# A hybrid encoder layer: early products from GpSimd to VectorE in pieces, whole-tile activations in halves, x^T staged apart, and the last scores behind the first U tile

## The chip, the cores and the metric

The kernel runs on one core of a Trainium2 chip. The metric is the device time of one execution in microseconds. The kernel before takes 2114.77 us, the median of 3 runs (2113.43 to 2115.89). Engines are named as the profile names them: PE is TensorE (PEld its weight loads), DVE is VectorE, ACT is ScalarE, POOL is GpSimd, and SP is SyncE, which here issues most of the DMAs.

## The reference: one layer on 256 tokens

There are 256 tokens of width 2048, in float32. Cut to what matters:

```
xn   = rms_norm(h, mix_norm_g)
q, k, v, g, xb, yb = split(xn @ w_in)          # six parts of 1024 columns
q, k = rotary(q), rotary(k) * 128**-0.5
ret  = silu(g) * head_group_norm(chunkwise_retention(q, k, v))   # 8 heads of 128

xc   = causal_conv4(xb)                         # RG-LRU, 8 blocks of 128 channels
r, i = sigmoid(xc @ w_rg + b_rg), sigmoid(xc @ w_ig + b_ig)
log_a = 8 * r * log_sigmoid(lru_lambda);  a = exp(log_a)
u    = sqrt(-expm1(2 * log_a)) * (i * xc)
hseq = scan(h_t = a_t * h_(t-1) + u_t)
lru  = rms_norm(hseq * gelu(yb), lru_norm_g)

h += concat(ret, lru) @ w_out
h += cross_attention(rms_norm(h), rms_norm(mem))   # w_xq, w_xk, w_xv, w_xo; 256 memory tokens
h += peer(rms_norm(h))    # 16384 experts: queries w_pq, scores against sub keys, top 16 twice,
                          # then gelu(u_e . x) and v_e of the chosen ones
return rms_norm(h, final_norm_g)
```

## The kernel before

**Weights.** All matrices are float32. SP streams them in half-blocks of 512 KB into four `raw` tiles. `split` (L115) makes two numbers of each weight: ACT casts `hi` (L119, four tiles), and VectorE subtracts to get `lo` (L120, three tiles). The activations are split in the same way: `xT`, `mT`, `cat`, `hT`, `xn` hold a high half [:T] and a low half [T:]. `w_mms` (L123) then issues for a half-block 8 matmuls of `hi` with both halves (L129, 512 columns) and 8 of `lo` with the high half (L131, 256 columns); in the second half-block the last `hi` matmul stands behind the `lo` ones. `col_block` makes a block of 128 output columns from two half-blocks, and `fold` adds the two halves of its result (ACT L153, VectorE L154). `xchunk` does the same with tokens on the partitions (L171, L172 for `hi`, L174 for `lo`).

**Stages.** In order: xb (8 blocks of w_xyg), yb (8 blocks), q, k, v (six chunks), gT (8 blocks), the memory keys w_xk (16 blocks into `kv`) and values w_xv, w_out, w_xq with attention, w_xo, the PEER queries w_pq (16 blocks into `qp`, each followed two blocks later by `sub_scores`), then the U and V tables.

**Side work.** Everything else comes from generators that a `Weave` runs: after each half-block `whalf` pumps `wv.rate` credits (1.1 in the early stages), and the generator at the head of the list is advanced until the credits are used; what it yields is the price of the step in credits. `prep_mem` and `lru` are queued in the yb stage, `retention` in the gT stage, `normed` and `route` later. Within this, a scheduler places the instructions on each engine, each engine then runs its own row in order, and waits where an operand or a buffer is not ready.

**The places that the change touches.** `load_x` (L237) brings a quarter of x^T through a `raw` tile; the four are mixed with the two half-blocks of the first weight block. `prep_mem` scales the memory tokens on GpSimd (L391, 128x1024, four times) and splits them with a gain (`split_gx`, ACT L222 and VectorE L223). In `lru`, GpSimd makes i * xc for all blocks (L329, 128x2048), ACT one square root of 128x2048 (L331); then for each block VectorE clips and inverts (L334, L335), GpSimd multiplies (L336), VectorE adds (L339); GpSimd multiplies the whole (L342), VectorE turns r into a (L344 to L346) and scans (L349, L350). Then ACT applies gelu to all of yb (L355), GpSimd multiplies (L357), ACT squares (L359), TensorE sums over channels (`lss`, L362), and `rsqrt` gives the scale. `lru_fin` applies it in eight products (L376) and splits into `cat`; it is called when the gT blocks are issued. In `retention`, ACT makes the sigmoid of gT (L471) and GpSimd gT * sg (L472), both 128x2048. `sub_scores` (L666) multiplies two 128x128 tiles of `qp` with the keys.

GpSimd's small products (L306, L399, L495, with the row scale of x) and its rotary steps (L427, L432) are not touched.

Of the kernel before, what the change touches and what calls it, by code (L numbers as in the profile page):

```python
# [14 lines left out]
ALU = mybir.AluOpType  # L15
AX = mybir.AxisListType

P = 128
# [53 lines left out]
def hybrid_layer_kernel(ctx: ExitStack, tc: tile.TileContext, a: dict, out: bass.AP, dbg=None):  # L72
# [163 lines left out]

    def load_x(q):  # L237
        t = raw_tile(a["xT"][q]).rearrange("p (k t) -> p k t", t=T)
        split_gx(xT, 4 * q, t, S_MIX)

# [14 lines left out]

    pt0 = mm("w0")
    load_x(0)
    r0 = raw_tile(a["w_xyg"][0, 0])
    load_x(1)
    whalf(0, None, xT, pt0, r0)  # L260
    load_x(2)
    r0 = raw_tile(a["w_xyg"][0, 1])
    load_x(3)
    whalf(1, None, xT, pt0, r0)
    fold(pt0, xb[:, 0, :])
# [11 lines left out]
    def lru():  # L277
# [49 lines left out]
        for g in range(8):  # L327
            A.activation(rt[:, g], rt[:, g], AF.Tanh, scale=lam[:, g:g + 1])
        G.tensor_tensor(it, it, xc, op=ALU.mult)  # L329
        yield 0.3  # L330
        A.activation(xc, rt, AF.Sqrt)  # L331
        yield 5.0
        for g in range(8):
            V.tensor_scalar(xc[:, g], xc[:, g], 1e-18, None, op0=ALU.max)  # L334
            V.reciprocal(q3[:, g], xc[:, g])  # L335
            G.tensor_tensor(q3[:, g], q3[:, g], rt[:, g], op=ALU.mult)  # L336
            yield 2.0
            if g:
                V.tensor_tensor(xc[:, g - 1], xc[:, g - 1], q3[:, g - 1], op=ALU.add)  # L339
        yield 0.4  # L340
        V.tensor_tensor(xc[:, 7], xc[:, 7], q3[:, 7], op=ALU.add)
        G.tensor_tensor(it, it, xc, op=ALU.mult)  # L342
        for g in range(8):
# [9 lines left out]
        while "yb" not in done:  # L353
            yield 3.0
        A.activation(yb, yb, AF.Gelu_apprx_tanh)  # L355
        yield 0.3
        G.tensor_tensor(xc, xc, yb, op=ALU.mult)  # L357
        yield 0.3
        A.activation(q3, xc, AF.Square)  # L359
        pt = sm("lss")  # L360
# [5 lines left out]
        yield 3  # L366
        lru_out.extend([xc, rl])
        done.add("lru")
# [3 lines left out]
    def lru_fin():  # L372
        xc, rl = lru_out
        cat["t"] = ct = big("cat")
        for g in range(8):
            V.scalar_tensor_tensor(xc[:, g], xc[:, g], small[:, S_LG + g:S_LG + g + 1], rl,  # L376
                                   op0=ALU.mult, op1=ALU.mult)
            if g % 4 == 3:
                split_x(ct, 8 + g - 3, xc[:, g - 3:g + 1])

# [3 lines left out]
    def prep_mem():  # L384
# [4 lines left out]
        for q in range(4):  # L389
            t = raw_tile(a["memT"][q]).rearrange("p (k t) -> p k t", t=T)  # L390
            G.tensor_tensor(t, t, rmb[:, None, :].to_broadcast([P, 4, T]), op=ALU.mult)  # L391
            yield 1.0
            split_gx(mT, 4 * q, t, S_MEM)
            yield 2.0
# [20 lines left out]
    def retention():  # L415
# [54 lines left out]
        sg = kt.rearrange("p a (b c) -> p (a b) c", c=T)  # L470
        A.activation(sg, gT, AF.Sigmoid)  # L471
        G.tensor_tensor(gT, gT, sg, op=ALU.mult)  # L472
        yield 0.3
        ct = cat["t"]
# [165 lines left out]
    def normed():  # L640
# [5 lines left out]
        for kb in range(0, KB + 2, 2):  # L646
# [8 lines left out]
            if prev:  # L655
# [3 lines left out]
                yield 0.8  # L659
            prev = nxt  # L660
        for tt in range(TT):
            V.scalar_tensor_tensor(h[tt], h[tt], r2[:, tt:tt + 1], gbc, op0=ALU.mult, op1=ALU.mult)
            yield 2.2
            G.dma_start(hn[tt * P:(tt + 1) * P, :], h[tt])
# [254 lines left out]
    def u_chunk(i):  # L919
        act = acts[i] = tp.tile([P, 8, T], F32, tag="act", name=f"act{i}", bufs=LEAD)  # L920
        for c in range(8):
            pt = mm("U")
            for j in range(2):
                whalf(j, a["U"][8 * i + c, j], xn, pt)
                tick(2 * c + j)
# [366 lines left out]
    for b in range(2, KB):  # L1292
        col_block(a["w_pq"], b, hT2, qp[b // 8][:, b % 8, :])
        sub_scores(b - 2)
    for b in (KB - 2, KB - 1):
        sub_scores(b)
# [146 lines left out]
```

## Time and profile before

| | |
|---|---|
| time, median of 3 runs (us) | 2114.77 (2113.43 to 2115.89) |
| the profiled execution: its own time / span (us) | 2121.89 / 2120.1 |
| mean granted TensorE clock | 0.984 |
| ACT / POOL busy, share of the span | 49% / 19% |
| DMA mean | 256 GB/s |

The stages as the trace has them, from the start of the span: xb to 58 us, yb to 110, q, k, v to 251, gT to 309, w_xk to 430, the PEER queries from about 820 to 913, the U blocks from there. A row of the timeline gives the start, the duration (of the group, where instructions of one form follow each other: x8), the engine, the line, the operation and out<-in; in brackets stands the idle time of the engine ahead of it and what released it. TensorE's granted clock falls after some of its idle times, and matmuls then take longer: `hi` matmuls that are issued 0.23 us apart at full clock are then up to 0.43 apart.

### The profile page before, as it was taken

To read this page: it belongs to the slowest core of one execution; us is meant where nothing else is said; L and a number is where in the kernel's file an instruction comes from. 1 tells how busy PE (TensorE), PEld (TensorE's weight loads), DVE (VectorE), ACT (ScalarE), POOL (GpSimd) and SP (SyncE) were. 2 spreads that over 40 slices of the span, in tenths; PEclk is the share of its full clock that TensorE was granted. 3 is DMA by queue.
4 is the path that set the end of the run, shared out by engine and by line. 5 is a ranking of instruction groups with operands and counts; after the bars stand their busy time and mean duration, and the time that the engine had idled before them with its cause. 6 is when DMAs were issued, how large, how long until landed. Compare 5 with 4: busy or idle time off the path is not lost. (4 is left out here: it accounts for less than half of the span.)

```text
span 2120.1 us, 29007 instructions
## 1 busy us (share of the span) xinstructions
PE 2042.2 (96%) x10452; PEld 1731.5 (82%) x10452; DVE 1701.4 (80%) x2421; ACT 1036.5 (49%) x1592; POOL 393.0 (19%) x211
## 2 busy tenths in 40 slices
PE   8999998999999999999999989999999999988997
PEld 6878787888888888888899978888888888766785
DVE  6857867644554457999997769999999999989897
ACT  6465343444444455554578853434434444433334
POOL 0303212000000000000000002323233332464342
PEclk9999999999999999999999979999999999999999
DMA  8675554566664467555676569999999999999874
GB/s 276 234 224 166 161 189 156 158 190 192 187 187 131 138 187 284 167 177 180 189 275 201 174 221 344 374 386 395 373 363 339 347 382 414 377 362 402 320 257 162
DMA packets 155014, 542.91 MB, mean 256 GB/s; under 512 B 17136, under 2 KB 44400, under 8 KB 136560
## 3 DMA queue, kind: packets, MB, share of 16 engines
q1 hardware_dynamic: 132832, 400.48, 56.2%
q0 software_dynamic: 22032, 140.53, 16.7%
q8 instruction: 82, 1.34, 0.3%
q14 instruction: 68, 0.56, 0.1%
HBM read 541.99 MB, written 18.87 MB: 265 GB/s over the span
## 5 line engine op out<-in xcount | busy, mean ns | idle before, releaser
L120 DVE TENSOR_TENSOR lo<-raw,hi 128x1024 fp32r<-128x1024 f32 x396 | 490.5, 1242 | 279.7 <-PE xc L174 135.1
L119 ACT CAST hi<-raw 128x1024 fp32r<-128x1024 f32 x396 | 414.9, 1050 | 305.6 <-PE xc L172 143.8
L1083 ACT CAST hi<-raw 128x1024 fp32r<-128x1024 f32 x272 | 283.7, 1049 | 266.9 <-DMA raw<-in_V_dram 88.8
L129 PE MATMUL U<-xn,hi 128*128 128x512 f32 x1536 | 403.5, 399 | 7.8 <-ACT hi L119 6.1
L1089 DVE TENSOR_TENSOR lo<-raw,hi 128x1024 fp32r<-128x1024 f32 x272 | 327.7, 1219 | 25.5 <-issue 17.1
L129 PEld LDWEIGHTS U<-xn,hi 128*128 128x128 f32 x1536 | 278.8, 191 | 58.4 <-ACT hi L119 6.2
L1126 POOL DMA_INDIRECT gat<-in_Us_dram,idx x69 | 114.9, 1665 | 684.9 <-DVE gat L1143 419.2
L131 PEld LDWEIGHTS U<-xn,lo 128*128 128x128 f32 x1536 | 212.6, 192 | 16.3 <-DVE lo L1089 1.3
L131 PE MATMUL U<-xn,lo 128*128 128x256 f32 x1536 | 220.8, 285 | 0.4 <-DVE lo L1089 0.4
L1143 DVE SCALAR_TENSOR_TENSOR gat<-gat,h 128x2048 f32<-128x2048 f32 x69 | 157.5, 2283 | 10.3 <-DMA gat<-in_Us_dram,idx 10.3
L944 PE MATMUL acc<-hi,ah 128*128 128x512 f32 x384 | 149.7, 390 | 1.5 <-DVE foldu L928 1.5
L945 PE MATMUL acc<-hi,al 128*128 128x512 f32 x384 | 149.4, 389 | 0.0
L129 PE MATMUL wb<-hT,hi 128*128 128x512 f32 x448 | 119.8, 401 | 0.0
L1126 POOL DMA_INDIRECT gat<-in_Vs_dram,idx x39 | 90.3, 2317 | 128.9 <-DVE hh L1151 111.4
L947 PE MATMUL acc<-lo,ah 128*128 128x512 f32 x384 | 103.4, 391 | 5.4 <-DVE lo L120 3.5
L129 PE MATMUL wb<-xT,hi 128*128 128x512 f32 x368 | 94.8, 399 | 9.8 <-ACT hi L119 9.8
L129 PEld LDWEIGHTS wb<-hT,hi 128*128 128x128 f32 x448 | 81.3, 189 | 14.1
L1151 DVE SCALAR_TENSOR_TENSOR hh<-gat,coef,hh 128x2048 f32<-128x2048 f32 x39 | 91.4, 2344 | 0.1
L947 PEld LDWEIGHTS acc<-lo,ah 128*128 128x128 f32 x384 | 71.6, 188 | 22.5 <-DVE lo L120 4.8
L129 PEld LDWEIGHTS wb<-xT,hi 128*128 128x128 f32 x368 | 67.0, 190 | 23.0 <-ACT hi L119 10.9
L944 PEld LDWEIGHTS acc<-hi,ah 128*128 128x128 f32 x384 | 72.1, 188 | 16.6 <-DVE foldu L928 1.8
L945 PEld LDWEIGHTS acc<-hi,al 128*128 128x128 f32 x384 | 72.1, 188 | 15.0
(410 smaller groups left out, 3722.6 us busy)
## 6 DMA issues: line engine op xcount, KB each, us to landing
raw<-in_U_dram SPq DMA_DIRECT2D x192, 512.0 KB, 4.9
raw<-in_V_dram SPq DMA_DIRECT2D x192, 512.0 KB, 7.7
raw<-in_w_xyg_dram SPq DMA_DIRECT2D x48, 512.0 KB, 4.4
raw<-in_w_qkv_dram SPq DMA_DIRECT2D x48, 512.0 KB, 3.8
raw<-in_w_xk_dram SPq DMA_DIRECT2D x32, 512.0 KB, 3.6
raw<-in_w_xv_dram SPq DMA_DIRECT2D x32, 512.0 KB, 3.6
raw<-in_w_out_dram SPq DMA_DIRECT2D x32, 512.0 KB, 3.5
raw<-in_w_xq_dram SPq DMA_DIRECT2D x32, 512.0 KB, 3.5
```

Source lines behind the costliest of these rows:

```text
L119: A.copy(hi, raw)
L120: V.tensor_tensor(lo, raw, hi.bitcast(F32), op=ALU.subtract)
L129: PE.matmul(pt, hi[:, ks], xt[:, kb, :], start=(kb == 0), stop=(kb == KB - 1))
L131: PE.matmul(pt[:, :T], lo[:, ks], xt[:, kb, :T], start=False, stop=False)
L944: PE.matmul(pt, ah[:, c, t_], hi[:, w], start=(first and c == 0), stop=False)
L945: PE.matmul(pt, al[:, c, t_], hi[:, w], start=False, stop=False)
L947: PE.matmul(pt, ah[:, c, t_], lo[:, w], start=False, stop=(last and c == 7))
L1083: A.copy(his[t], raws[t])
L1089: V.tensor_tensor(los[t], raws[t], his[t].bitcast(F32), op=ALU.subtract)
L1126: G.indirect_dma_start(gat, None, a[tab], bass.IndirectOffsetOnAxis(ap=idx[tt][:, k:k + 1], axis=0), bounds_check=NS - 1, oob_is_err=False)
L1143: V.scalar_tensor_tensor(gat, gat, 1.0, h[0], op0=ALU.mult, op1=ALU.mult, accum_out=dots[tt, k0][:, k:k + 1])
L1151: V.scalar_tensor_tensor(hh[tt], gat, coef[tt, k0][:, k:k + 1], hh[tt], op0=ALU.mult, op1=ALU.add)
```

## The change

What it does, edit by edit:

- x^T is loaded into the tiles of yb and gT, which are not yet in use, by `stage_x`; no x^T goes through a `raw` tile. The order of splits at the start is written out anew.
- The memory products (L391 before, L397 after) run on VectorE, and yield 1.4 instead of 1.0.
- In `lru`, the three products on GpSimd become pieces of one block on VectorE; the square root and the gelu come in halves (128x1024), the gate product and the Square in quarters (128x512). The eight final products move from `lru_fin` into `lru`, behind `rsqrt`, with a yield each.
- In `retention`, the sigmoid and the gating product come in halves, the product on VectorE.
- In the PEER stage, `normed` is pumped until `xn` is done, the first half-block of the first U tile is issued, and the last two `sub_scores` follow it; `u_chunk` starts with the second half-block there.

```diff
-    def load_x(q):
-        t = raw_tile(a["xT"][q]).rearrange("p (k t) -> p k t", t=T)
-        split_gx(xT, 4 * q, t, S_MIX)
+    def stage_x(q):
+        t = (yb, gT)[q // 2][:, 4 * (q % 2):4 * (q % 2) + 4, :]
+        nc.sync.dma_start(t, a["xT"][q].rearrange("p (k t) -> p k t", t=T))
+        return t
...
-    load_x(0)
-    r0 = raw_tile(a["w_xyg"][0, 0])
-    load_x(1)
-    whalf(0, None, xT, pt0, r0)
-    load_x(2)
-    r0 = raw_tile(a["w_xyg"][0, 1])
-    load_x(3)
-    whalf(1, None, xT, pt0, r0)
+    x4 = [stage_x(0)]
+    r0 = [raw_tile(a["w_xyg"][0, 0])]
+    x4.append(stage_x(1))
+    r0.append(raw_tile(a["w_xyg"][0, 1]))
+    x4 += [stage_x(2), stage_x(3)]
+    for j in range(2):
+        split_gx(xT, 8 * j, x4[2 * j], S_MIX)
+        hl = split(r0[j])
+        split_gx(xT, 8 * j + 4, x4[2 * j + 1], S_MIX)
+        w_mms(j, *hl, xT, pt0)
+        wv.pump(wv.rate)
...
-        G.tensor_tensor(it, it, xc, op=ALU.mult)
-        yield 0.3
-        A.activation(xc, rt, AF.Sqrt)
-        yield 5.0
+            V.tensor_tensor(it[:, g], it[:, g], xc[:, g], op=ALU.mult)
+            yield 0.5
+        for g in range(0, 8, 4):
+            A.activation(xc[:, g:g + 4], rt[:, g:g + 4], AF.Sqrt)
+            yield 1.0
...
-            G.tensor_tensor(q3[:, g], q3[:, g], rt[:, g], op=ALU.mult)
-            yield 2.0
-            if g:
-                V.tensor_tensor(xc[:, g - 1], xc[:, g - 1], q3[:, g - 1], op=ALU.add)
-        yield 0.4
-        V.tensor_tensor(xc[:, 7], xc[:, 7], q3[:, 7], op=ALU.add)
-        G.tensor_tensor(it, it, xc, op=ALU.mult)
+            V.tensor_tensor(q3[:, g], q3[:, g], rt[:, g], op=ALU.mult)
+            yield 1.6
+            V.tensor_tensor(xc[:, g], xc[:, g], q3[:, g], op=ALU.add)
+            V.tensor_tensor(it[:, g], it[:, g], xc[:, g], op=ALU.mult)
+            yield 0.8
...
-        A.activation(yb, yb, AF.Gelu_apprx_tanh)
-        yield 0.3
-        G.tensor_tensor(xc, xc, yb, op=ALU.mult)
-        yield 0.3
-        A.activation(q3, xc, AF.Square)
+        for g in range(0, 8, 4):
+            A.activation(yb[:, g:g + 4], yb[:, g:g + 4], AF.Gelu_apprx_tanh)
+            yield 1.0
+        for g in range(0, 8, 2):
+            V.tensor_tensor(xc[:, g:g + 2], xc[:, g:g + 2], yb[:, g:g + 2], op=ALU.mult)
+            A.activation(q3[:, g:g + 2], xc[:, g:g + 2], AF.Square)
+            yield 0.7
...
         for g in range(8):
             V.scalar_tensor_tensor(xc[:, g], xc[:, g], small[:, S_LG + g:S_LG + g + 1], rl,
                                    op0=ALU.mult, op1=ALU.mult)
-            if g % 4 == 3:
-                split_x(ct, 8 + g - 3, xc[:, g - 3:g + 1])
+            yield 0.5
...
-            G.tensor_tensor(t, t, rmb[:, None, :].to_broadcast([P, 4, T]), op=ALU.mult)
-            yield 1.0
+            V.tensor_tensor(t, t, rmb[:, None, :].to_broadcast([P, 4, T]), op=ALU.mult)
+            yield 1.4
...
-        A.activation(sg, gT, AF.Sigmoid)
-        G.tensor_tensor(gT, gT, sg, op=ALU.mult)
-        yield 0.3
+        for g in range(0, 8, 4):
+            A.activation(sg[:, g:g + 4], gT[:, g:g + 4], AF.Sigmoid)
+            yield 1.0
+            V.tensor_tensor(gT[:, g:g + 4], gT[:, g:g + 4], sg[:, g:g + 4], op=ALU.mult)
+            yield 1.0
...
+        done.add("xn")
...
-            pt = mm("U")
-            for j in range(2):
+            pt = mm("U") if i or c else pt0
+            for j in range(0 if i or c else 1, 2):
...
+    while "xn" not in done:
+        wv.pump(1.0)
+    pt0 = mm("U")
+    whalf(0, a["U"][0, 0], xn, pt0)
     for b in (KB - 2, KB - 1):
         sub_scores(b)
```

Three places where the order of instructions differs. First VectorE where the memory tokens are prepared, in the yb stage, before the change: `rmb` is the row scale of the memory tokens, and what follows it is

```order
L210 COPY rmb<-bc 128x256
L120 TENSOR_TENSOR lo<-raw,hi 128x1024
L223 SCALAR_TENSOR_TENSOR mT<-raw,small,mT 128x256 x4
L154 TENSOR_TENSOR yb<-wb,fold 128x256
L223 SCALAR_TENSOR_TENSOR mT<-raw,small,mT 128x256 x4
L120 TENSOR_TENSOR lo<-raw,hi 128x1024 x2
```

and after it, from the same instruction on:

```order
L210 COPY rmb<-bc 128x256
L397 TENSOR_TENSOR raw<-raw,rmb 128x1024 x2
L223 SCALAR_TENSOR_TENSOR mT<-raw,small,mT 128x256 x4
L154 TENSOR_TENSOR yb<-wb,fold 128x256
L120 TENSOR_TENSOR lo<-raw,hi 128x1024 x2
L223 SCALAR_TENSOR_TENSOR mT<-raw,small,mT 128x256 x3
```

The first `lo` behind `rmb` now stands behind two products and four mT steps.

Second VectorE at the end of the gT stage and the start of w_xk (`lt` holds the RG-LRU's tiles, `ro` are the rotary's products, `cat` is the input of w_out), before, from the last step of `rsqrt` to the first late `lo`:

```order
L189 TENSOR_TENSOR lt<-lt,rq_s 128x256
L120 TENSOR_TENSOR lo<-raw,hi 128x1024
L154 TENSOR_TENSOR gT<-wb,fold 128x256
L376 SCALAR_TENSOR_TENSOR lt<-lt,small 128x256 x4
L426 TENSOR_TENSOR ro_2528<-q,cs 128x512
L428 TENSOR_TENSOR ro_2529<-q,cs 128x512
L215 TENSOR_TENSOR cat<-lt,cat 128x4x256
L429 TENSOR_TENSOR q<-ro_2528,ro_2529 128x8x64
L376 SCALAR_TENSOR_TENSOR lt<-lt,small 128x256
L430 TENSOR_TENSOR ro_2528<-q,cs 128x512
L376 SCALAR_TENSOR_TENSOR lt<-lt,small 128x256 x3
```

(two rotary products and the `lo` follow) and after, from the same step of `rsqrt` on:

```order
L189 TENSOR_TENSOR lt<-lt,rq_s 128x256
L436 TENSOR_TENSOR ro_2554<-q,cs 128x512
L373 SCALAR_TENSOR_TENSOR lt<-lt,small 128x256 x8
L215 TENSOR_TENSOR cat<-lt,cat 128x4x256
L432 TENSOR_TENSOR ro_2640<-q,cs 128x512
L215 TENSOR_TENSOR cat<-lt,cat 128x4x256
L434 TENSOR_TENSOR ro_2641<-q,cs 128x512
L154 TENSOR_TENSOR kv<-wb,fold 128x256
L435 TENSOR_TENSOR q<-ro_2640,ro_2641 128x8x64
L120 TENSOR_TENSOR lo<-raw,hi 128x1024
```

No `lo` stands between `rsqrt` and the eight products any more: the whole of `rsqrt`, the products, both splits into `cat` and a `kv` fold are ahead of the next one. On TensorE the mean square moved with it, from ahead of the last gT block to behind it, as the third place shows; before:

```order
L362 MATMUL lss<-lt,ones 128x256 x8
L129 MATMUL wb<-xT,hi 128x512 x8
L131 MATMUL wb<-xT,lo 128x256 x8
L129 MATMUL wb<-xT,hi 128x512 x7
L131 MATMUL wb<-xT,lo 128x256 x8
L129 MATMUL wb<-xT,hi 128x512
L129 MATMUL wb<-mT,hi 128x512 x8
```

and after, from the last matmul with x^T to the late `lo`:

```order
L129 MATMUL wb<-xT,hi 128x512
L367 MATMUL lss<-lt,ones 128x256 x8
L129 MATMUL wb<-mT,hi 128x512 x8
L131 MATMUL wb<-mT,lo 128x256 x8
L129 MATMUL wb<-mT,hi 128x512 x7
L131 MATMUL wb<-mT,lo 128x256 x8
L129 MATMUL wb<-mT,hi 128x512 x9
L131 MATMUL wb<-mT,lo 128x256 x8
L129 MATMUL wb<-mT,hi 128x512 x23
```

A whole gT block passed the mean square, and 23 `hi` matmuls are now in a row ahead of the next `lo`. At the first U tile, TensorE's row before was

```order
L669 MATMUL sub<-kq,qp_6488 128x128 x4
L129 MATMUL U<-xn,hi 128x512 x3
L669 MATMUL sub<-kq,qp_6488 128x128 x2
L129 MATMUL U<-xn,hi 128x512 x5
L131 MATMUL U<-xn,lo 128x256 x8
```

and is after

```order
L678 MATMUL sub<-kq,qp_6508 128x128 x2
L129 MATMUL U<-xn,hi 128x512 x8
L131 MATMUL U<-xn,lo 128x256 x8
L678 MATMUL sub<-kq,qp_6508 128x128 x4
L129 MATMUL U<-xn,hi 128x512 x7
```

The last four score matmuls went behind the `hi` and `lo` matmuls of the first U half-block.

More of the change, by code (lines that the diff above doesn't have):

```diff
@@ L366, in lru @@
         yield 3
-        lru_out.extend([xc, rl])
+        for g in range(8):
+            V.scalar_tensor_tensor(xc[:, g], xc[:, g], small[:, S_LG + g:S_LG + g + 1], rl,
+                                   op0=ALU.mult, op1=ALU.mult)
+            yield 0.5
+        lru_out.append(xc)
         done.add("lru")
@@ L372, in lru_fin @@
     def lru_fin():
-        xc, rl = lru_out
+        xc = lru_out[0]
         cat["t"] = ct = big("cat")
-        for g in range(8):
-            V.scalar_tensor_tensor(xc[:, g], xc[:, g], small[:, S_LG + g:S_LG + g + 1], rl,
-                                   op0=ALU.mult, op1=ALU.mult)
-            if g % 4 == 3:
-                split_x(ct, 8 + g - 3, xc[:, g - 3:g + 1])
+        for g in (0, 4):
+            split_x(ct, 8 + g, xc[:, g:g + 4])
     rm = cp.tile([P, TT], F32, name="rm")
```

## The prediction

> **What bounds the kernel now.** I read first the page's busy shares, then the windows by stage, then TensorE's waits, and last the timeline around each long wait. The page's first part (engine, busy us, share of the span) and two windows (stretch, its length, then busy time and instructions of PE, PEld, DVE, ACT, POOL, and the granted clock):
>
> ```profile
> PE 2042.2 (96%) x10452; PEld 1731.5 (82%) x10452; DVE 1701.4 (80%) x2421; ACT 1036.5 (49%) x1592; POOL 393.0 (19%) x211
> ```
>
> ```profile
> 0.00:440.00 440.00, 408.98 (x2087) 345.46 (x2088) 315.55 (x442) 220.88 (x299) 79.33 (x52) 0.98 0.61 195
> ```
>
> ```profile
> 168.00:251.00 83.00, 79.40 (x340) 65.18 (x339) 76.97 (x83) 38.05 (x42) 22.74 (x10) 0.96 0.55 168
> ```
>
> TensorE is the bound: what other engines do costs time only where it leaves TensorE idle, or slow after idling. In the first 440 us it idles 440 - 408.98 = 31.0 us, and this is what the early edits can win. The waits up to 1000 us (who waited for whom, total us, times, longest) say where:
>
> ```profile
> PE wb L129 <- ACT hi L119: 9.8, 5, 3.8
> ...
> PE wb L131 <- DVE lo L120: 5.6, 3, 3.8
> PE sub L669 <- DVE qp L154: 4.0, 2, 3.5
> PE xc L174 <- DVE lo L120: 3.8, 2, 3.6
> PE retT L484 <- DVE q L479: 2.6, 1, 2.6
> ```
>
> These are a few single stalls of about 3.5 us, not a rate that is too low. I call their places A to G in order of time and cost each from its own rows of the timeline (start, duration, engine, line, what; in brackets the idle time before and who ended it).
>
> **A, the start.** An ACT step on x^T, the cast for block 1, and TensorE's first matmuls of block 1:
>
> ```profile
> 14.20 1.71 ACT L222 ACTIVATE xT<-raw,small 128x256 fp32r<-128x256 f32 x4 [0.67 <-DMA raw<-in_xT_dram]
> 17.32 1.03 ACT L119 CAST hi<-raw 128x1024 fp32r<-128x1024 f32 x1
> 18.41 2.14 PE L129 MATMUL wb<-xT,hi 128*128 128x512 f32 x8 [0.66 <-ACT hi L119]
> ```
>
> The last x^T load waits for a raw buffer and ACT waits 0.67 us for it; the cast ends at 18.35 and TensorE follows at 18.41. With places of its own x^T is there earlier, and later weight loads start a little sooner too: I take 0.9. Zero is the low end, should ACT's own row of casts decide; twice that, about 1.6, if TensorE's other short waits ahead of 18.41 shrink as well.
>
> **B, preparing the memory tokens.** GpSimd's products, VectorE's `lo` and its mT and x^T steps (groups: count, busy us, mean ns), and TensorE's three waits:
>
> ```profile
> L391 POOL TENSOR_TENSOR raw<-raw,rmb 128x1024 f32<-128x1024 f32 x4 | 11.9, 2995 | 8.3 <-DVE rmb L210 3.8 <-DMA raw<-in_memT_dram 2.4 <-ACT mT L222 2.2
> ```
>
> ```profile
> L120 DVE TENSOR_TENSOR lo<-raw,hi 128x1024 fp32r<-128x1024 f32 x135 | 169.8, 1264 | 95.0 <-PE xc L174 30.3 <-ACT hi L119 27.9 <-issue 20.0
> ...
> L223 DVE SCALAR_TENSOR_TENSOR mT<-raw,small,mT 128x256 fp32r<-128x256 f32 x16 | 12.0, 804 | 2.5 <-ACT mT L222 2.5
> ...
> L223 DVE SCALAR_TENSOR_TENSOR xT<-raw,small,xT 128x256 fp32r<-128x256 f32 x16 | 6.6, 482 | 3.0 <-ACT xT L222 3.0
> ```
>
> ```profile
> 99.11 1.89 PE L129 MATMUL wb<-xT,hi 128*128 128x512 f32 x7 [3.24 <-ACT hi L119]
> ...
> 101.43 1.22 PE L131 MATMUL wb<-xT,lo 128*128 128x256 f32 x8 [0.43 <-DVE lo L120]
> ...
> 107.13 1.88 PE L129 MATMUL wb<-xT,hi 128*128 128x512 f32 x7 [1.46 <-ACT hi L119]
> ```
>
> The three sum to 5.1 us. ACT's cast stands in line behind mT, and mT behind GpSimd's 2.995 us. On VectorE a product of this size costs what a `lo` of the same shape does, 1.264 us. But two of them (2.5 us) and four mT (4 x 0.482 = 1.9, the undisturbed price) now stand ahead of a weight `lo` that went first before. Some of these 4.4 us are hidden by `lo` being ready early; I estimate that 1.2 of stall stays, and take a gain of 3.9. If the whole 4.4 shows, 0.7 is left of the gain; 5.1 is the other end, and up to 1 more if the short waits up to 115 us go.
>
> **C, the RG-LRU beside q, k and v.** GpSimd's whole product, VectorE's two small instructions under it, TensorE's wait, and the first matmul after the slow stretch; the fifth row is an undisturbed run of TensorE from later, and the groups are prices:
>
> ```profile
> 213.37 5.45 POOL L342 TENSOR_TENSOR lt<-lt 128x2048 f32<-128x2048 f32 x1 [0.60 <-DVE lt L341]
> ...
> 214.28 4.89 DVE L344 TENSOR_SCALAR lt<-lt 128x256 f32<-128x256 f32 x2
> ...
> 221.97 2.07 PE L174 MATMUL xc<-lo,xT 128*128 128x512 f32 x4 [3.60 <-DVE lo L120]
> ...
> 228.21 0.39 PE L171 MATMUL xc<-hi,xT 128*128 128x512 f32 x1
> ```
>
> ```profile
> 388.67 2.23 PE L129 MATMUL wb<-mT,hi 128*128 128x512 f32 x9
> ```
>
> ```profile
> L344 DVE TENSOR_SCALAR lt<-lt 128x256 f32<-128x256 f32 x8 | 6.4, 831 | 0.0
> ...
> L334 DVE TENSOR_SCALAR lt<-lt 128x256 f32<-128x256 f32 x8 | 4.3, 550 | 0.0
> ...
> L349 DVE TENSOR_TENSOR lt<-lt 128x256 f32<-128x256 f32 x8 | 3.0, 411 | 0.0
> ...
> L346 DVE TENSOR_SCALAR lt<-lt 128x256 f32<-128x256 f32 x8 | 2.2, 274 | 0.0
> ```
>
> Beside L342 two small instructions took 4.89 us, so the next `lo` was late and TensorE waited 3.60. From 221.97 to 228.21 it then issued 16 matmuls in 6.24 us; undisturbed they are 0.23 apart (nine in 2.23, the last one's own length aside), so 3.7 us, and the slow stretch cost 2.5. Together 6.1.
> After the change VectorE does 24 more pieces here (8 each for L329, L336, L342) at L349's 0.411: 9.9 us. What GpSimd inflated comes back: against L346's undisturbed 0.274, L344 gives 8 x 0.557 = 4.5 and L334 8 x 0.276 = 2.2. So VectorE's 76.97 us of 83 become about 80.2: still under, and in even steps, with 3 us to spare. I take 6.0; the low end, 2, leaves one stall of that kind.
>
> **D, the gate product.** The same picture with ACT between: GpSimd's product, ACT's Square behind it, TensorE waiting for a cast behind the Square:
>
> ```profile
> 257.06 6.58 POOL L357 TENSOR_TENSOR lt<-lt,yb 128x2048 f32<-128x2048 f32 x1 [38.23 <-DVE lt L350]
> ```
>
> ```profile
> 263.67 1.91 ACT L359 ACTIVATE lt<-lt 128x2048 f32<-128x2048 f32 x1 [9.24 <-POOL lt L357]
> ```
>
> ```profile
> 267.72 2.92 PE L129 MATMUL wb<-xT,hi 128*128 128x512 f32 x7 [3.77 <-ACT hi L119]
> ```
>
> The wait is 3.77 and seven matmuls at 0.23 plus a tail would be 1.8, so 2.92 holds 1.1 of slowness, and I estimate 0.6 more in the slow `lo` matmuls behind (C's four took 2.07): 5.5 in all. In pieces of 128x512, half a `lo`, ACT waits for one product of some 0.6 us at a time and the casts come between. I take 5.5; 4 if one wait of 1.5 us stays.
>
> **E, the hand-over to the memory keys.** TensorE's matmuls of the mean square, its two waits here and the stretched `hi` matmuls between them, and the price of a reciprocal on VectorE:
>
> ```profile
> 300.09 3.61 PE L362 MATMUL lss<-lt,ones 128*128 128x256 f32 x16
> ```
>
> ```profile
> 323.98 2.07 PE L131 MATMUL wb<-mT,lo 128*128 128x256 f32 x8 [3.78 <-DVE lo L120]
> 325.85 4.95 PE L129 MATMUL wb<-mT,hi 128*128 128x512 f32 x13
> ...
> 339.67 1.22 PE L131 MATMUL wb<-mT,lo 128*128 128x256 f32 x8 [1.43 <-DVE lo L120]
> ```
>
> ```profile
> L335 DVE RECIPROCAL lt<-lt 128x256 f32<-128x256 f32 x8 | 13.9, 1739 | 0.0
> ```
>
> Thirteen matmuls would be 3.1, so 4.95 holds 1.8 of slowness, eight `lo` at 1.22 (the last row) make 2.07 hold 0.85, and the loss here is 3.78 + 1.8 + 0.85 + 1.43 = 7.9. The change does not remove it, it moves it. The RG-LRU's steps ask for more credits than the stages pump, so the order puts the mean square behind the last gT block (3.61 us of TensorE's work that used to stand ahead of that block), and the reciprocal square root with all eight final products comes between two `lo` of w_xk. Added there: a reciprocal (1.74), five steps and a fold at about 0.41 (L349's), a split of `lo`'s shape (1.26) and a rotary step of half its width (0.6): 6.1 us. Off there: TensorE has 23 `hi` matmuls queued instead of 11, 12 x 0.23 = 2.8 of cover, and GpSimd's inflation of the final products, which are no longer strewn between its rotary steps (0.3 each by the two L223 rows, 2.6 for eight). So the stall stays about as long: I take -0.5, from -3 to +3.
>
> [...]
>
> **F, retention's end.** VectorE's copy of 16 columns beside GpSimd's gating product L472, and TensorE:
>
> ```profile
> 388.18 3.18 DVE L464 COPY gn_v<-gn_mv 128x16 f32<-128x16 f32 x1
> ```
>
> ```profile
> 394.43 0.35 PE L484 MATMUL retT<-ident,q 128*128 128x128 f32 x1 [2.57 <-DVE q L479]
> ...
> 395.07 2.91 PE L129 MATMUL wb<-mT,hi 128*128 128x512 f32 x6
> ```
>
> The wait is 2.57; six matmuls at 0.23 plus a tail are 1.5, so 1.4 of slowness, together 4.0. The product becomes two halves on VectorE, each of a `lo`'s size, and the transposes come some steps later in TensorE's order. I take 4.0; 2.5 if only the wait goes.
>
> **G, the first U tile.** TensorE's wait for the last scores, and VectorE afterwards:
>
> ```profile
> 919.01 1.22 PE L669 MATMUL sub<-kq,qp 128*128 128x128 f32 x4 [3.48 <-DVE qp L154]
> ```
>
> ```profile
> 923.96 1.23 DVE L120 TENSOR_TENSOR lo<-raw,hi 128x1024 fp32r<-128x1024 f32 x1 [1.87 <-PE U L131]
> ```
>
> The order now puts 8 `hi` and 8 `lo` matmuls ahead of the scores' wait where 3 `hi` stood. TensorE could win the 3.48 and the slowness behind it, but VectorE is full here: its one idle spot is this 1.87 us, so the stage cannot move up by more than that and what else of slack is in its rows, which I put at half a microsecond: 2.4. The side work that the U blocks carry also starts later against them and is paid at the stage's end, about 1 us a step. I take 1.1, from -1 to 2.4.
>
> **Sum.** 0.9 + 3.9 + 6.0 + 5.5 - 0.5 + 4.0 + 1.1 = 20.9 us. The profiled execution took 2121.89 us (span 2120.1), 7.1 above the median of the runs; it should come to about 2101, and the median, 2114.77, to 2093.9.
>
> **The rivals.**
> *E goes too.* If the stall at the hand-over vanishes with the others, 7.9 + 0.5 = 8.4 more: 2085.5. For it: less of GpSimd beside the rotary steps. Against: VectorE has 6.1 us more between the two `lo` than before.
> *E grows.* the added 6.1 us are covered by the 2.8 alone: the stall of 3.78 nearly doubles, with 2.65 more of slowness, and B keeps 2 us more: 2093.9 + 3.6 + 2.65 + 2.0 = 2102.2. For it: rotary steps on GpSimd still fall among the products. Against: fewer do than before.
> *VectorE takes C's gain.* Its steps come unevenly and C's stall returns, with half of B's and D's gains: 2093.9 + 6.0 + 2.0 + 2.7 = 2104.6. For it: 3 us to spare in 83.
> *Slower: VectorE becomes the bound beside q, k and v.* Here the pieces, each of which waits for the one before, cost far more than L349's, and VectorE sets the stage's end. All gains but C are 14.9; VectorE would have to take 83 + 14.9 = 97.9 us, and with the 6.7 us of inflation gone that is (97.9 - 70.3)/24 = 1.15 us a piece. From there on the kernel is slower; at 1.5, between L344's mean of 0.831 and the 2.45 that each of its two took beside L342, it is 70.3 + 36 = 106.3, a loss of 23.3, and 2114.8 + 23.3 - 14.9 = 2123.2. Against: L349 is the same operation in the same shape at 0.411.
> [...]
>
> **How the numbers follow.** Chances: the forecast 0.52, E goes 0.19, E grows 0.11, C returns 0.14, slower 0.04. The range from 2084 to 2106 holds the forecast with its ends (2089 to 2099), E goes but for its edge, and the two poorer cases but for some: about 0.83. A difference of 0.2%, about 4.2 us, is what a measurement of this kernel can tell from no change. Faster by more: all but the slower rival and the worst of the poor cases, 0.91; within it 0.05; slower 0.04.
>
> **What would show it.** Right: in the profile after, no TensorE wait above 1 us between 200 and 275 us and none at the retention transposes; L344's successor at about 0.28 mean; a wait of 2 to 5 us for `lo` in the first blocks of w_xk, with a low clock behind it; TensorE's idle time up to 440 us at about 14 us. Wrong: a VectorE without idle time between 168 and 251 us with waits of `xc` on `lo`; or w_xk without a wait; or more idle time in the U stage than was won at its start.

## The result, and the profile after

The changed kernel takes 2093.82 us (median of 4 runs, 2092.84 to 2099.48) against 2115.33 us of the kernel before in the same comparison (median of 4, 2113.43 to 2118.17): ratio 0.9904, 95% interval 0.9889 to 0.9918. That is 21.5 us less; 20.9 were forecast. The profiled execution took 2099.48 us with a span of 2097.7, so it stands 5.7 us above its median, as the one before stood 7.1 above its own.

The page's first part after the change, and its first 440 us (the columns as before):

```profile
PE 2030.7 (97%) x10452; PEld 1721.0 (82%) x10452; DVE 1698.7 (81%) x2455; ACT 1039.0 (50%) x1600; POOL 342.0 (16%) x195
```

```profile
0.00:440.00 440.00, 420.06 (x2167) 355.93 (x2168) 320.49 (x482) 231.85 (x316) 34.70 (x36) 0.99 0.63 203
```

The span became 22.4 us shorter, and half of it is idle time: TensorE idled 2120.1 - 2042.2 = 77.9 us and now 2097.7 - 2030.7 = 67.0. The other 11.5 us are busy time: the same 10452 matmuls kept TensorE busy for less long, at a mean granted clock of 0.993 against 0.984 before. The waits up to 1000 us, to be held against the five of before:

```profile
PE w L129 <- ACT hi L119: 8.1, 1, 8.1
PE wb L131 <- DVE lo L120: 6.2, 3, 3.8
PE sub L678 <- DVE qp L154: 2.1, 1, 2.1
PE wb L129 <- ACT hi L119: 2.1, 3, 1.7
PE qkT L449 <- POOL q L438: 1.7, 1, 1.7
```

The first row is the start of the kernel. The waits `xc` on `lo` and `retT` on `q` are gone, and `wb` on `hi` fell from 9.8 to 2.1; `wb` on `lo` has grown from 5.6 to 6.2, and `qkT` on GpSimd's `q` is new. TensorE's idle time in equal windows, each the window's length less its busy time, puts the places side by side:

| window, us | place | before | after | forecast gain, slowness included |
|---|---|---|---|---|
| 0 to 60 | A | 10.30 | 8.92 | 0.9 |
| 60 to 116 | B | 5.41 | 4.02 | 3.9 |
| 116 to 235 | C | 3.60 | 0.00 | 6.0 |
| 235 to 285 | D | 3.77 | 0.00 | 5.5 |
| 285 to 365 | E | 5.37 | 7.01 | -0.5 |
| 365 to 440 | F | 2.57 | 0.00 | 4.0 |
| 880 to 940 | G | 3.98 | 2.13 | 1.1 with the next row |
| 1030 to 1070 | G, later | 0.00 | 2.20 | |

The differences sum to 10.7 us, all but 0.2 of the idle time that went. For C, these are VectorE's groups between 116 and 240 us (count, busy us, mean ns):

```profile
L333 DVE TENSOR_TENSOR lt<-lt 128x256 f32<-128x256 f32 x8 | 3.3, 414 | 2.7 <-ACT lt L329 2.7
...
L347 DVE TENSOR_SCALAR lt<-lt 128x256 f32<-128x256 f32 x8 | 2.1, 287 | 0.0
L339 DVE TENSOR_SCALAR lt<-lt 128x256 f32<-128x256 f32 x8 | 2.0, 287 | 0.1
```

The moved pieces cost 0.414 us each; the two steps that stood at 0.831 and 0.550 beside GpSimd are at 0.287. For E, the rows show TensorE at the start of w_xk, then VectorE's final products and GpSimd beside them:

```profile
302.24 5.41 PE L129 MATMUL wb<-mT,hi 128*128 128x512 f32 x23
...
311.52 1.41 PE L131 MATMUL wb<-mT,lo 128*128 128x256 f32 x8 [3.77 <-DVE lo L120]
...
315.01 0.47 PE L449 MATMUL qkT<-ident,q 128*128 128x128 f32 x1 [1.66 <-POOL q L438]
```

```profile
291.57 0.42 DVE L154 TENSOR_TENSOR gT<-wb,fold 128x256 f32<-128x256 f32 x1
294.06 0.42 DVE L182 TENSOR_SCALAR rq_m<-lss 128x256 f32<-128x256 f32 x1 [2.07 <-PE lss L367]
...
300.59 5.34 DVE L373 SCALAR_TENSOR_TENSOR lt<-lt,small 128x256 f32<-128x256 f32 x8
...
310.26 1.21 DVE L120 TENSOR_TENSOR lo<-raw,hi 128x1024 fp32r<-128x1024 f32 x1
```

```profile
300.81 1.43 POOL L438 TENSOR_TENSOR q<-ro,ro 128x512 f32<-128x512 f32 x1 [3.71 <-DVE ro L436]
302.19 1.47 POOL L433 TENSOR_TENSOR ro<-q,cs 128x512 f32<-128x512 f32 x1
```

From 294.06, when the mean square is there, VectorE passes 16 us of other work before the next `lo` at 310.26; the wait of 3.78 is back as 3.77, and behind it stands a second one, for GpSimd's rotary. The inputs of that mean square were done long before: VectorE's last gate product ended at 240.4, and from 250 to 290 VectorE is busy 19.5 of 40 us.

### The profile page after: what moved, and what is told of

Its sections match the earlier page's. It is cut to its first block, busy times and chain, and to the rows that moved or that the text cites. A ratio compares the mean times of both kernels' runs of the same rounds, so it can differ in the third digit from the quotient of the medians.

```text
span 2097.7 us, 29005 instructions
## 1 busy us (share of the span) xinstructions
PE 2030.7 (97%) x10452; PEld 1721.0 (82%) x10452; DVE 1698.7 (81%) x2455; ACT 1039.0 (50%) x1600; POOL 342.0 (16%) x195
## 4 chain that ended last, share of the span: by engine, by line
PE 77%; DVE 14%; DMA 4%; issue 3%; ACT 1%; POOL 1%; ACTq 0%; DVEq 0%; SPq 0%; POOLq 0%
PE U L129 13%; PE wb L129 8%; PE U L131 7%; PE xc L171 6%; PE xc L172 6%; PE xc L174 6%; PE acc L956 5%; PE acc L953 5%; PE acc L954 5%; PE wb L131 4%; DVE lo L120 4%; PE G L884 2%; PE V L956 2%; PE V L953 2%; PE V L954 2%
## 5 line engine op out<-in xcount | busy, mean ns | idle before, releaser
L1135 POOL DMA_INDIRECT gat<-in_Us_dram,idx x69 | 122.2, 1771 | 682.6 <-DVE gat L1152 424.5
L1135 POOL DMA_INDIRECT h<-in_Vs_dram,idx x33 | 70.7, 2144 | 108.3 <-DVE hh L1160 101.5
```

Of the source, the lines that this page charges most:

```text
L1135: G.indirect_dma_start(gat, None, a[tab], bass.IndirectOffsetOnAxis(ap=idx[tt][:, k:k + 1], axis=0), bounds_check=NS - 1, oob_is_err=False)
```

## The experiments

The idle time of the eight windows, for all runs (0.00 is left blank; where a run has the changed kernel's code in a window, its number shows how far that window varies by itself):

| run | 0 to 60 | 60 to 116 | 116 to 235 | 235 to 285 | 285 to 365 | 365 to 440 | 880 to 940 | 1030 to 1070 |
|---|---|---|---|---|---|---|---|---|
| before | 10.30 | 5.41 | 3.60 | 3.77 | 5.37 | 2.57 | 3.98 | |
| after | 8.92 | 4.02 | | | 7.01 | | 2.13 | 2.20 |
| e1_pool_pieces | 8.22 | 1.48 | 5.06 | | 7.90 | | 2.16 | 2.18 |
| e2_whole_v | 8.04 | 0.87 | | | 6.51 | | 2.08 | 2.37 |
| e3_rate24 | 8.85 | 1.39 | | | 8.65 | | 1.96 | 2.20 |
| e4_rot_v | 8.98 | 1.07 | | | 4.74 | | 2.22 | 0.93 |
| e5_spread | 8.43 | 2.62 | | | 5.38 | | 2.02 | 0.97 |
| e6_mem_pool | 8.85 | 4.51 | | | 6.15 | | 2.12 | 0.88 |
| e7_ret_pool | 8.04 | 1.99 | | | 6.02 | 2.57 | 1.89 | 2.19 |
| e8_scores_first | 8.75 | 1.38 | | | 5.83 | | 4.03 | |
| e9_x_raw | 8.60 | 1.67 | | | 5.43 | | 2.08 | 0.88 |
| e10_all | 8.20 | 1.50 | | | 0.23 | | 2.15 | 0.99 |

Single runs of one kernel lie up to 13 us apart (the kernel before, 2111.01 to 2124.11 in one comparison), and the intervals of the kernels that undo one part (e1 and e6 to e9) all overlap that of the changed kernel. So for a part of a few us the traces decide, and the times only say whether they agree. The traces vary as well, and here mostly E: in the seven kernels with the changed kernel's code there (after, e1, e2, e6 to e9) its window idles 5.43 to 7.90.

Much of the spread lies late. The end of VectorE's 32nd `foldu` step, in the U blocks and behind the last window of the table, is a mark that every trace has. The kernel before reaches it at 1112.1 us and the changed one at 1092.4, which is 19.7 of the 22.4 us. From the mark to the end it is 1008.0 and 1005.3, and in the ten kernels below, which have the changed kernel's code there, 998.1 to 1011.4.

**The engine or the size of the pieces?** Two kernels take the two halves of the RG-LRU edit apart. The first keeps the pieces and gives them back to GpSimd:

```diff
-            V.tensor_tensor(it[:, g], it[:, g], xc[:, g], op=ALU.mult)
+            G.tensor_tensor(it[:, g], it[:, g], xc[:, g], op=ALU.mult)
...
-            V.tensor_tensor(q3[:, g], q3[:, g], rt[:, g], op=ALU.mult)
+            G.tensor_tensor(q3[:, g], q3[:, g], rt[:, g], op=ALU.mult)
...
-            V.tensor_tensor(it[:, g], it[:, g], xc[:, g], op=ALU.mult)
+            G.tensor_tensor(it[:, g], it[:, g], xc[:, g], op=ALU.mult)
...
-            V.tensor_tensor(xc[:, g:g + 2], xc[:, g:g + 2], yb[:, g:g + 2], op=ALU.mult)
+            G.tensor_tensor(xc[:, g:g + 2], xc[:, g:g + 2], yb[:, g:g + 2], op=ALU.mult)
```

> The changed kernel with the RG-LRU's products (i * xc, q3 * rt, it * xc, xc * yb) back on GpSimd, but in the new pieces. Theory one, the engine decides (VectorE stands still beside a GpSimd product): VectorE's small steps beside the pieces are stretched again (around 0.5 instead of 0.28 us), the stretch between 168 and 250 us has TensorE waits of 2 to 6 us in all, so 2096 to 2100 us where the changed kernel has 2093.8. Theory two, only the size of the pieces decides: no such waits, 2093 to 2095.

Measured: 2097.33 us (2096.68 to 2105.99), ratio to before 0.9923 (0.9897 to 0.9950). TensorE's wait in C, then GpSimd's and VectorE's groups there:

```profile
PE xc L174 <- DVE lo L120: 5.1, 3, 2.4
```

```profile
L341 POOL TENSOR_TENSOR lt<-lt 128x256 f32<-128x256 f32 x8 | 11.8, 1479 | 12.8 <-DVE lt L340 12.8
```

```profile
L343 DVE TENSOR_TENSOR lt<-lt 128x256 f32<-128x256 f32 x8 | 5.0, 621 | 3.1 <-POOL lt L341 3.1
L339 DVE TENSOR_SCALAR lt<-lt 128x256 f32<-128x256 f32 x8 | 3.6, 490 | 0.0
```

The loss in C is back, in three waits instead of one, and VectorE's steps are stretched again (0.287 to 0.490). Theory one holds for C. D does not come back: the gate product in quarters on GpSimd costs TensorE nothing. The second kernel keeps VectorE and drops the pieces of the three products that were whole before:

```diff
-            V.tensor_tensor(it[:, g], it[:, g], xc[:, g], op=ALU.mult)
             yield 0.5
+        V.tensor_tensor(it, it, xc, op=ALU.mult)
...
-            V.tensor_tensor(it[:, g], it[:, g], xc[:, g], op=ALU.mult)
             yield 0.8
+        V.tensor_tensor(it, it, xc, op=ALU.mult)
...
+        V.tensor_tensor(xc, xc, yb, op=ALU.mult)
         for g in range(0, 8, 2):
-            V.tensor_tensor(xc[:, g:g + 2], xc[:, g:g + 2], yb[:, g:g + 2], op=ALU.mult)
```

> The changed kernel with i * xc, it * xc and xc * yb on VectorE as whole products of 128x2048, the credits the same. Theory one, the engine decides: a whole product takes about 8 x 0.33 = 2.7 us, less than the 4.89 and 6.58 us that GpSimd's held the others up, and a lo is ready early enough: at most 1 us of wait in each place, 2093 to 2096. Theory two, the size decides: the waits of before come back with 2 to 4 us in each of the two places, 2098 to 2102.

Measured: 2093.79 us (2089.23 to 2096.37), ratio 0.9898 (0.9869 to 0.9926), no idle time in C or D. The whole product on VectorE:

```profile
L345 DVE TENSOR_TENSOR lt<-lt 128x2048 f32<-128x2048 f32 x1 | 2.3, 2280 | 0.0
```

It takes 2.28 us where GpSimd's took 5.45. So in C the engine makes the gain and the pieces add nothing that shows; in D either edit is enough, as long as ACT's gelu and Square stay in parts. Both kernels keep those parts, and what they do alone was not run.

**The hand-over, E.** The first attempt only pumps more credits in the gT stage, so that the mean square comes ahead of its last blocks:

```diff
+    wv.rate = 2.4
     for b in range(8):
         if b == 0:
             wv.add(retention())
...
+    wv.rate = RA
     lru_fin()
```

> The changed kernel with 2.4 credits a half-step instead of 1.1 through the gT stage, so that the mean square, its reciprocal root and the final products stand ahead of the last gT blocks and the rotary steps begin there. Theory one, the hand-over is late because credits ran out while VectorE had half its time free from 245 to 290: the 10 us lost at the start of w_xk fall to 3 to 5, 2087 to 2090. Theory two, the loss there is set by VectorE's and GpSimd's work itself and only moves: 2092 to 2095.

Measured: 2097.40 us (2095.98 to 2097.75), ratio 0.9911 (0.9884 to 0.9939), above the ranges of both theories, and E's idle time went up, to 8.65: a miss for theory one as it was put. Two of TensorE's waits, and what VectorE does meanwhile:

```profile
PE wb L131 <- DVE lo L120: 4.4, 3, 2.9
PE qkT L449 <- POOL k L438: 4.0, 1, 4.0
```

```profile
295.08 0.69 DVE L434 TENSOR_TENSOR ro<-q,cs 128x512 f32<-128x512 f32 x1 [3.15 <-POOL q L438]
```

The higher rate also pulled in the rotary steps, one behind the other, and in VectorE's row a `lo` now stood behind a rotary step that waited 3.15 us for GpSimd. More room was not enough; what is put into it matters. The second attempt leaves the rate and takes GpSimd out of the rotary steps:

```diff
-                G.tensor_tensor(m3, x[:, :, 0], s, op=ALU.mult)
+                V.tensor_tensor(m3, x[:, :, 0], s, op=ALU.mult)
...
-                G.tensor_tensor(x[:, :, 1], m1, m3, op=ALU.add)
+                V.tensor_tensor(x[:, :, 1], m1, m3, op=ALU.add)
```

> The changed kernel with the rotary's two GpSimd steps on VectorE too, so that GpSimd is still around the hand-over. Theory one, the hand-over's lump of VectorE work makes the wait: the eight final products come down from 5.34 us to about 3.2, but three more rotary steps of 0.6 stand in the same place, so the wait stays at 3 to 4.5 us and the time within 2092 to 2096. Theory two, GpSimd beside VectorE makes it: the loss falls by 4 or more, 2089 or less.

Measured: 2092.19 us (2089.53 to 2100.22), ratio 0.9882 (0.9853 to 0.9911). VectorE's products, and TensorE's wait behind them:

```profile
297.44 3.26 DVE L373 SCALAR_TENSOR_TENSOR lt<-lt,small 128x256 f32<-128x256 f32 x8
```

```profile
307.50 1.22 PE L131 MATMUL wb<-mT,lo 128*128 128x256 f32 x8 [2.68 <-DVE lo L120]
```

The eight products came down from 5.34 to 3.26 as theory one had it, yet the wait fell to 2.68, below its 3 to 4.5: E's idle time went from 7.01 to 4.74. Each theory has a part: beside the changed kernel's own trace, GpSimd is worth 1.1 us of that wait and 2.3 of E's idle time. That the rest is the lump is only argued so far. The third attempt spreads the lump and leaves the rotary on GpSimd:

```diff
-                yield 1.6
+                yield 0.8
...
-            yield 1.0
+            yield 0.3
...
-            yield 0.7
+            yield 0.2
...
+        wv.rate = RA
         rl = rt[:, 0]
...
-            yield 0.5
+            yield 0.9
...
+    wv.rate = 3.0
     for b in range(8):
```

(the scan, the gelu halves, the gate quarters; then ahead of `rsqrt`, behind each final product, and ahead of the gT blocks)

> The changed kernel with 3 credits a half-step in the gT stage up to the reciprocal root and 1.1 from there, smaller prices for the scan, gelu and gate steps and 0.9 for each final product, so that the eight products stand in three groups among the lo of the gT stage, and the rotary steps are not packed. Theory one, the loss at the start of w_xk is VectorE work in one lump ahead of a lo: the 10 us there fall to 2 to 4 and nothing comes in their place, 2086 to 2089. Theory two, the work itself costs TensorE that time wherever it stands: the loss moves into the gT stage, 2092 to 2097.

Measured: 2090.91 us (2087.19 to 2092.27), ratio 0.9870 (0.9839 to 0.9901), between the two ranges. The gT stage took all of the moved work at no cost (0.00 idle from 235 to 285), which is against theory two, but E kept 5.38, more than theory one said and only just under the 5.43 of the best of those seven kernels. TensorE still waits there for `lo` (3.7 us in two waits) and for a copy on ACT (1.7). VectorE is busy without a break ahead of both late `lo`, and some of its rotary steps beside GpSimd are stretched:

```profile
290.64 1.78 DVE L435 TENSOR_TENSOR ro<-q,cs 128x512 f32<-128x512 f32 x1
...
294.69 1.78 DVE L437 TENSOR_TENSOR ro<-q,cs 128x512 f32<-128x512 f32 x1
```

where L435 takes 0.68 at 301.74 us, with no GpSimd step running; beside the two rows above GpSimd's L434 runs from 290.14 (1.74 us) and from 294.31 (1.62). The last kernel spreads the lump and takes GpSimd out, with a rotary step in three parts of a credit each:

```diff
-                G.tensor_tensor(m3, x[:, :, 0], s, op=ALU.mult)
+                V.tensor_tensor(m3, x[:, :, 0], s, op=ALU.mult)
+                yield 1.0
...
+                yield 1.0
...
-                yield 2.5
-                G.tensor_tensor(x[:, :, 1], m1, m3, op=ALU.add)
+                V.tensor_tensor(x[:, :, 1], m1, m3, op=ALU.add)
+                yield 1.0
```

> The spread version (3 credits a half-step in the gT stage up to the reciprocal root, final products in three groups) with all rotary steps on VectorE in three parts of a credit each. Theory one: what the spread version still loses at the start of w_xk, 7.7 us, comes from VectorE steps stretched to 1.8 us beside GpSimd's rotary steps, ahead of a lo; without GpSimd the loss falls to 2 to 4 and the time to 2085 to 2088. Theory two: VectorE's added eight steps of 0.6 us are as long as the stretching was, the loss stays at 6 to 9, 2089 to 2093.

Measured: 2085.62 us (2082.87 to 2087.84), ratio 0.9855 (0.9831 to 0.9879), the lowest median of all; its interval overlaps that of e5_spread and lies below that of the changed kernel. Its window from 285 to 365 us:

```profile
285.00:365.00 80.00, 79.77 (x483) 69.56 (x482) 59.68 (x100) 40.52 (x58) 1.85 (x2) 1.00 0.56 173
```

0.23 us idle at a granted clock of 1.00, below theory one's 2 to 4, with as much VectorE work as before (59.68 against 58.27 in the changed kernel). So E's loss was not work for which there was no room; it was how the work was placed, in a lump, and steps that GpSimd held up (1.78 us for 0.68 in e5_spread). This kernel changes the rotary's engine and its pacing together, so it does not say what each of the two is worth beside the spread.

**The other parts, each undone by itself.** The memory products on GpSimd again, with their old price of 1.0:

```diff
-            V.tensor_tensor(t, t, rmb[:, None, :].to_broadcast([P, 4, T]), op=ALU.mult)
-            yield 1.4
+            G.tensor_tensor(t, t, rmb[:, None, :].to_broadcast([P, 4, T]), op=ALU.mult)
+            yield 1.0
```

> The changed kernel with the memory products back on GpSimd. Theory one: TensorE loses 5 to 6 us between 85 and 112 us again, where the new order loses 2 to 5, so 2095 to 2098. Theory two, the products' engine is without effect there, since raw buffers held by the memory tokens set the pace: the loss stays at 2 to 5 and the time within 2092 to 2095.

Measured: 2099.83 us (2097.23 to 2101.57), ratio 0.9918 (0.9886 to 0.9949).

```profile
98.29 3.35 PE L129 MATMUL wb<-xT,hi 128*128 128x512 f32 x7 [3.68 <-ACT hi L119]
```

The wait that B had before is back (3.24 there), this time with stretched matmuls behind it (3.35 for the 1.89 of before). From 85 to 112 us TensorE idles 4.30 us, and with those 1.5 the loss is the 5 to 6 of theory one; the window's 4.51 stands above the 0.87 to 2.62 of nine kernels, but only just above the changed kernel's own 4.02. The time is 2 us above theory one's range. Retention's gating whole and on GpSimd again:

```diff
-        for g in range(0, 8, 4):
-            A.activation(sg[:, g:g + 4], gT[:, g:g + 4], AF.Sigmoid)
-            yield 1.0
-            V.tensor_tensor(gT[:, g:g + 4], gT[:, g:g + 4], sg[:, g:g + 4], op=ALU.mult)
-            yield 1.0
+        A.activation(sg, gT, AF.Sigmoid)
+        G.tensor_tensor(gT, gT, sg, op=ALU.mult)
+        yield 0.3
```

> The changed kernel with the sigmoid of gT and the gating product whole again, the product on GpSimd. Theory one: the copy of 16 columns on VectorE takes about 3 us again and TensorE waits 2 to 3 us for the normalised q, with 1 to 2 of slow clock behind: 2097 to 2099. Theory two, the wait of before came from the place of the transposes in TensorE's order alone: at most 1 us of wait, 2093 to 2095.

Measured: 2098.64 us (2095.87 to 2102.04), ratio 0.9916 (0.9886 to 0.9947); theory one, and both the copy and TensorE's wait are back at what they were before the change (3.18 and 2.57):

```profile
371.60 3.18 DVE L470 COPY gn_v<-gn_mv 128x16 f32<-128x16 f32 x1
```

```profile
377.85 0.30 PE L490 MATMUL retT<-ident,q 128*128 128x128 f32 x1 [2.57 <-DVE q L485]
```

The sigmoid is whole again here too, so this kernel does not separate ACT's halves from the engine of the product. The last scores ahead of the first U half-block again:

```diff
-    while "xn" not in done:
-        wv.pump(1.0)
-    pt0 = mm("U")
-    whalf(0, a["U"][0, 0], xn, pt0)
...
-            pt = mm("U") if i or c else pt0
-            for j in range(0 if i or c else 1, 2):
+            pt = mm("U")
+            for j in range(2):
```

> The changed kernel with the last two score products ahead of the first U half-block again. Theory one, VectorE is full there and gives back what TensorE wins: the wait for qp is 3 to 4 us again with 2 of slow clock, but waits for lo later in the U stage are 2 to 3 us fewer, so 2094.5 to 2097. Theory two, TensorE's order alone decides: 2098 to 2101.

Measured: 2097.05 us (2093.40 to 2098.77), ratio 0.9898 (0.9866 to 0.9929); the window at the first U tile and the later one:

```profile
880.00:940.00 60.00, 55.97 (x310) 48.64 (x310) 57.51 (x163) 30.78 (x48) 0.00 (x0) 0.94 0.57 176
1030.00:1070.00 40.00, 40.00 (x242) 35.58 (x241) 38.63 (x77) 21.46 (x40) 4.42 (x4) 1.00 0.77 270
```

4.03 us idle with a clock of 0.94, and nothing at 1030 to 1070, where every kernel with the new order idles 0.9 to 2.4: theory one, with the time at the upper edge of its range. And x^T through raw tiles again, as in the code that the diff of the change shows with a minus:

> The changed kernel with x^T through raw tiles again, in the order of before. Theory one, x^T's places of its own are what block 1 gains from: TensorE loses 5.5 to 6 us up to 60 us instead of 4.0 to 4.9, 2094.5 to 2096. Theory two, the start is set by ACT's own row and the loads: 4 to 5 us are lost there as well, 2093 to 2094.5.

Measured: 2098.56 us (2095.34 to 2101.97), ratio 0.9922 (0.9893 to 0.9952). TensorE idles 8.60 us in the first 60, inside the 8.04 to 8.98 of the runs with places of their own, and block 1 starts where the changed kernel has it:

```profile
13.56 1.71 ACT L222 ACTIVATE xT<-raw,small 128x256 fp32r<-128x256 f32 x4
```

```profile
17.78 2.11 PE L129 MATMUL wb<-xT,hi 128*128 128x512 f32 x8
```

ACT's wait of 0.67 for the last load, on which A's term stood, is not there although the load goes through a raw tile: in that execution it landed earlier. So the trace is for theory two. The median lies above both ranges, but the start is not the reason: this trace, of the fastest of the four executions (2095.34), reaches the mark in the U blocks at 1088.7 us, 3.7 ahead of the changed kernel's. What made the other executions longer stays open.

## Why the prediction was right

**C, D and F**, 15.5 of the 20.9 us, came as worked out. VectorE did its 24 pieces at 0.414 to 0.417 (0.411 was taken), L344's and L334's inflation went back to 0.287, and no wait of `xc` was left. All 9.9 us of idle time in their windows went; the other 5.6 were put down to slow matmuls, which were not measured apart, but the granted clock in these windows is 1.00, after 0.97, 0.97 and 0.98. That GpSimd's steps held VectorE's up here is shown by e7_ret_pool for a whole product (the copy at 3.18 us, 0.17 in the changed kernel) and by e1_pool_pieces for pieces (L339 at 0.490, 0.287 there). One reason given was wrong without harm: D's pieces were taken for the cure, and whole products on VectorE (e2_whole_v) do as well.

**E** was put at -0.5 with ends of -3 and +3; TensorE's idle time there grew by 1.6, which is less than the window varies by itself (5.43 to 7.90). The order was read rightly (23 `hi` in a row, then a wait for `lo`, 3.77 after 3.78). The term "GpSimd's inflation of the final products" had the right sign but was too large. Before the change the eight took 7.0 us:

```profile
L376 DVE SCALAR_TENSOR_TENSOR lt<-lt,small 128x256 f32<-128x256 f32 x8 | 7.0, 923 | 0.0
```

After it they take 5.34, since two GpSimd rotary steps still fall among them, and 3.26 with no GpSimd beside them (e4_rot_v): 1.7 us came off, not 2.6. What the sum left out is that TensorE itself waits for a rotary step, 1.66. That credits ran out while VectorE stood half idle was seen only in the trace after.

**B** was put at 3.9. The profiled execution shows 1.4: the wait for `lo` behind products and mT was there (1.64, about 1.2 forecast), and a second one that the sum did not have, since a cast waited for a load:

```profile
95.94 1.22 PE L131 MATMUL wb<-xT,lo 128*128 128x256 f32 x8 [1.64 <-DVE lo L120]
...
104.44 1.89 PE L129 MATMUL wb<-xT,hi 128*128 128x512 f32 x7 [1.70 <-ACT hi L119]
```

```profile
103.34 1.04 ACT L119 CAST hi<-raw 128x1024 fp32r<-128x1024 f32 x1 [4.28 <-DMA raw<-in_w_xyg_dram]
```

In the nine other kernels with this code the window idles 0.87 to 2.62, a gain of 2.8 to 4.5 against the one trace of before, so the term was about right and this one execution poor.

**A** came out as 1.4 for 0.9 forecast, but e9_x_raw has the same without the edit: the reason did not hold, no gain of x^T's places is shown, and the term was met by luck.

**G** was put at 1.1 under a cap from VectorE. TensorE won 1.85 us of idle time and the stretched matmuls behind the wait, which were these before (the score matmuls ahead of them start at 919.01):

```profile
919.89 2.48 PE L129 MATMUL U<-xn,hi 128*128 128x512 f32 x5
922.16 1.76 PE L131 MATMUL U<-xn,lo 128*128 128x256 f32 x8
923.76 1.77 PE L129 MATMUL U<-xn,hi 128*128 128x512 f32 x7
```

From start to start the four score matmuls took 0.88, the five `hi` 2.27 and the eight `lo` 1.60; behind the wait of the changed kernel four score matmuls take 0.47 and eight `lo` 0.94, and five `hi` at 0.23 are 1.15. That is 2.2 more won. TensorE gave back 2.20 between 1030 and 1070: about 1.8. The cap was the right thought, and the term a little low.

The sum was nearer than its terms: B and E came out poorer, A and G better. And 2.7 of the profiled 22.4 us lie behind the mark in the U blocks, within what kernels with the same code vary there by themselves, so a part of the agreement of 21.5 with 20.9 is luck. The granted clock from 1000 to 1270 us is 0.96 before and 0.98 after; over the whole span it is 0.984 and 0.993, and 0.989 and 0.988 in e4_rot_v and e9_x_raw.

Two of the signs named ahead did not come as wished. TensorE idles 19.9 us up to 440 us, not about 14. The idle part of the forecast's own terms is 14.3 of the 31.0, which would leave 16.7, and the second waits of B (1.70) and E (1.66) are about the rest. And one sign of being wrong, more idle time in the U stage than was won at its start, came true by a little (2.20 against 1.85); what makes G a gain is the slowness that went. The rival "E goes too" is not what happened here, but it is what e10_all does: its 2085.62 stands beside the rival's 2085.5, a nearness that is in part chance, since the kernel before took 2117.50 in that comparison. The rival "E grows" adds 3.6 us, where its own 6.1 less 2.8 would be 3.3.

## What to carry to other kernels

Where the bound engine waits in a few lumps of 3 to 4 us, look for a long instruction on one engine under which small ones of another take long, as two small VectorE steps took 4.89 us beside GpSimd's product of 5.45 here; try it on that other engine before cutting it into pieces (whole on VectorE it took 2.28). Side work that is paced by prices should be checked in the trace against the time at which its inputs are ready: here 50 us lay between a sum's inputs and the sum, and all of it then fell into one lump. A gain from an edit is shown only when the edit alone, undone, takes it back.

## What the runs showed of the hardware

Small VectorE steps took longer beside GpSimd's products. The copy of 16 columns (L464) of the kernel before, from 388.18 us on, took 3.18 and ended at 391.36, where GpSimd's product ended at 391.33:

```profile
386.35 4.98 POOL L472 TENSOR_TENSOR gT<-gT,k 128x2048 f32<-128x2048 f32 x1 [42.93 <-ACT k L471]
```

In the changed kernel, where GpSimd is not busy from 365 to 440 us, the same copy takes 0.17:

```profile
376.57 0.17 DVE L470 COPY gn_v<-gn_mv 128x16 f32<-128x16 f32 x1
```

In e7_ret_pool, with the product back on GpSimd, it takes 3.18 again. Like this copy, L339 has one tile as input: it took 0.490 beside GpSimd's pieces in e1_pool_pieces and 0.287 in the changed kernel.

Idle times of nearly one length on TensorE were followed by different granted clocks. The wait at the first U tile (2.13 and 2.17 us) was followed by undisturbed matmuls in the changed kernel (seven in 1.86 us, granted clock 1.00 from 880 to 940 us) and by stretched ones in e4_rot_v (2.95, granted clock 0.97):

```profile
900.89 0.71 PE L678 MATMUL sub<-kq,qp 128*128 128x128 f32 x4 [2.13 <-DVE qp L154]
...
901.36 1.86 PE L129 MATMUL U<-xn,hi 128*128 128x512 f32 x7
```

```profile
895.60 0.71 PE L678 MATMUL sub<-kq,qp 128*128 128x128 f32 x4 [2.17 <-DVE qp L154]
896.06 2.95 PE L129 MATMUL U<-xn,hi 128*128 128x512 f32 x7
```

Nor did the longer wait have the slower matmuls behind it: 3.24 us in the kernel before, in B, were followed by seven in 1.89, and 2.17 here by seven in 2.95. What decides between the two is not shown.
